# K in four loads, gates fetched two chunks ahead, output splits shared otherwise, and a reordered first stage, in a hybrid attention and retention layer

## The chip, the cores and the metric

The kernel runs on one core of one Trainium2 chip. The metric is the device time of one execution in microseconds (us). The kernel computes on TensorE (matrix products, called PE in the profile), VectorE (DVE), ScalarE (ACT) and GpSimd (POOL). SyncE (SP) issues every DMA, in program order: an issue that has to wait for a buffer holds up all issues behind it.

## The reference

One layer with two parallel branches on the same modulated input, for 1024 latent tokens and 128 context tokens (1152 in all, model width 1024, float32):

```python
mod = silu(cond) @ w_mod + b_mod                  # shift, scale, gate: 3 x 1024
h = layernorm(x) * (1 + scale) + shift
qa, ka, va, za, qr, kr, vr, zr = split(h @ w_in)
# attention, 8 heads: latent queries see 128 cached context keys and 1024 latent keys (rotated)
oa = (softmax(q1 k1') - lam * softmax(q2 k2')) v  # per head, then RMS norm and gain
oa = (oa * silu(za)) @ w_pa
# retention, 8 heads, forwards and backwards in chunks of 128, then layernorm and gain
orr = (orr * silu(zr)) @ w_pr
ga, gr = split(sigmoid(h @ w_gate + b_gate))
y = layernorm(alpha * x + gate * ((ga * oa + gr * orr) @ w_out)) * ln_g + ln_b
```

Outputs are y for both kinds of tokens, and the context's keys, values and retention states. The modulation (shift, scale, gate) differs between latent and context tokens, so each of its 1024 channels has two values, one per row of `cond`.

## The kernel before, in words

Products that must be accurate are made of three: a float32 operand is split into a high part, rounded by ScalarE (`hi_of`), and a low part, the remainder, subtracted by VectorE or GpSimd (`lo_of`); TensorE then adds high x high, high x low and low x high. In profile rows `whi` and `wlo` are the parts of a weight, `Y[:, 0]` and `Y[:, 1]` those of the modulated input h.

All instructions are put out in the order in which the Python code emits them, engine by engine. In the first stage this order is written out by hand. Afterwards a small planner (`Sched`) keeps an estimated clock of TensorE (`sch.t`) and of the other engines (`sch.e`), and lets several generators take turns: a stream of dense jobs (`dense`, one weight tile of 128 output columns each, in three chunks of 384 tokens, 24 matmuls per chunk) fills TensorE while other streams wait. `sch.later` puts a follow-up off until its estimated time; `sch.guard(tag, n)` calls pending follow-ups until fewer than n of that tag are left. Two PSUM buffers (`dn`) take the dense chunks in turn, so TensorE can run one chunk ahead of the engine that empties them.

The stages in order:

- First stage (`phase_h`). Nine tiles of x (128 tokens each) are loaded, normalised, transposed and kept as `xnT`. Beside this the modulation is computed. Channel blocks of 128: scale 0 and 1 and shift 0 and 1 are group 0 of `GS`, scale 2 and 3 group 1, scale 4 to 7 group 2. A group is made by `scale_k(g, k)` on TensorE (one float32 matmul per block k of the input, with the weights as the moving operand), copied by ScalarE (`scale_rows`), transposed, and added to the bias by VectorE (`scale_cols`, into `m1` or `sh`; rows `m<-tp,bm`). The shifts 2 to 7 are made by VectorE alone from row-wise weights (`by_rows`, rows `junk<-wm,scb`). `load_wk(g, k)` loads a group's weights, `load_shift(j)` the row-wise ones; many of these use `p0x`, a ring of six buffers shared with the x tiles, so a load waits until the tile six places earlier has been used. `mod(j)` then makes channel block j of h for all tokens: `hf` on ScalarE, its high part on ScalarE (rows `Y<-hf`), its low part on VectorE (rows `Y<-hf,Y`). After each `mod(k + 1)` TensorE multiplies block k with two weight tiles at once (`k_part`), high x high, low x high, high x low.
- Phase A: projections for retention and attention in the dense stream, with the retention cores beside it. Rotated keys go to DRAM (`Kd`), likewise queries (`Qh`, `Ql`) and values (`Vd`).
- Phase B: attention. For each head h and chunk c (four of 256 latent queries, then one of 128 context queries) `softmax_stream` loads the next chunk's queries (`load_q`), computes the scores into PSUM (`S`), their row maxima (`nm`) and exponentials (`E`). At chunk 1 of a head `load_k(h + 1)` loads the next head's K, 128 partitions x 2 x 1280 floats, into one of two K buffers. `pv_stream` multiplies with V, and `rms` normalises a finished head: a small store to `RSd`, read back broadcast as `rb`. Between these the dense stream runs gates (`g_job`, sigmoid gates stored to `Gd`) and the silu gates (`gate_out`, stored to `ORd` and `OAd` from buffers `goh`, `gol`).
- Phase D: merge. `pr_job(j)` multiplies the gated retention output (tiles `K`, `X`) with `w_pr`, three chunks for each of eight j; VectorE multiplies each chunk by its gate (rows `gt<-gt,dn`) and stores it to `Td`. `merge_in(0, j, c + 1)`, called when chunk c has been evacuated, loads the next gate chunk into one of two `gt` buffers. `pa_job(j)` does the same for attention, with two loads per chunk, the gate (`gt`) and the stored `Td` (`tz`). Beside it `ada_gate` makes the modulation's gate on VectorE (rows `junk<-gw,o_sb`, `gc`).
- Phase E: output. `w_out_split(n)` splits eight pieces of `w_out` into `Y` (no longer needed as input): pieces 0 to 3 are put out just before the last merge chunk, 4 to 7 after it. Even pieces get their low part from GpSimd, odd ones from VectorE. Then matmuls into `e`, the residual, the final layernorm and the stores.

Of the kernel before, what the change touches and what calls it, by code (L numbers as in the profile page):

```python
# [11 lines left out]
F32 = mybir.dt.float32  # L12
F32R = mybir.dt.float32r
AF = mybir.ActivationFunctionType
ALU = mybir.AluOpType
# [3 lines left out]
P = 128  # L19
D = 1024  # L20
KT = D // P
# [3 lines left out]
NH = 8  # L25
CW = 384
NC = NT // CW
# [112 lines left out]
def hybrid_step(ctx: ExitStack, tc: tile.TileContext, I: dict, O: dict):  # L140
# [61 lines left out]
    def dma(out, in_):  # L202
        nc.sync.dma_start(out=out, in_=in_)  # L203
# [159 lines left out]
    def phase_h(first, load_decays, decays_y):  # L363
# [3 lines left out]
        with es:  # L367
# [21 lines left out]
            def load_shift(j):  # L389
                t = wm["shift", j] = p0x("wm")  # L390
                dma(t, I["w_shift"][j])

            GS = ((0, 4), (0, 2), (2, 6))

            def load_wk(g, k):

                a, b = GS[g]
                n = 8 // (b - a)  # L400
                t = p0x("wk") if k == 6 or g == 1 else p0.tile([P, D], F32, tag="wk", name="wk", bufs=3)
                t = t.rearrange("p (k c) -> p k c", k=n)
                dma(t, I["w_scale_k" if g else "w_mod01"][k:k + n, :, a * P:b * P].rearrange("k p c -> p k c"))
                for i in range(n):
                    wm[g, k + i] = t[:, i, :]
# [2 lines left out]
            dma(ident, I["ident"])  # L408
            for i in range(NTILE):
                load_x(i)  # L410
                if i in (2, 4, 6):
                    load_wk(0, i - 2)
                if i == 4:
                    dma(bm, I["b_mod"])
                if i == 6:
                    load_wk(0, 6)
            junk = p0.tile([P, D], mybir.dt.bfloat16, name="junk")
            nc.gpsimd.memset(ones, 1.0 / P)
            nc.gpsimd.memset(mhalf, -0.5)
# [26 lines left out]
            def by_rows(j):  # L446
# [2 lines left out]
                    v_stt(junk, wm["shift", j], 1.0, scb[r], ALU.mult, ALU.mult, accum_out=sh[:, j, r:r + 1])  # L449
                v_ts(sh[:, j, :], sh[:, j, :], bm[:, j:j + 1], None, ALU.add)  # L450

            scale_ps = {}

            def scale_k(g, k):
# [13 lines left out]
            def scale_cols(g):  # L468

                n = GS[g][1] - GS[g][0]  # L470
                rows = rows_of[g]
                tp = psum_now("tp")
                for j in range(n):
                    nc.tensor.transpose(tp[:, 2 * j:2 * j + 2], rows[:, j * P:(j + 1) * P], ident[0:2, 0:2])
                    sch.t += 0.107
                for j0, dst, a, m, one in (((0, m1, 0, 2, 1.0), (2, sh, 0, 2, 0.0)), ((0, m1, 2, 2, 1.0),),
                                           ((0, m1, 4, 4, 1.0),))[g]:
                    c0 = 8 + a if one else a
                    v_stt(dst[:, a:a + m, :], tp[:, 2 * j0:2 * (j0 + m)].rearrange("p (j r) -> p j r", r=2), one,
                          bm[:, c0:c0 + m].rearrange("p (j o) -> p j o", o=1).to_broadcast([P, m, 2]),  # L480
                          ALU.add, ALU.add)
# [15 lines left out]
            for i in range(NTILE):  # L497
                if i + 2 < NTILE:
                    stats(i + 2)
                if i + 1 < NTILE:  # L500
                    normalise(i + 1)
                for g in range(2):
                    tp = psum_now("tp")
                    for k in range(4):
                        kk = g * 4 + k
                        tpose(tp[:, k * P:(k + 1) * P], xt[i][:, kk * P:(kk + 1) * P])
                    act(xnT[:, g * 4:(g + 1) * 4, i * P:(i + 1) * P],
                        tp.rearrange("p (k c) -> p k c", k=4))
                for k in ((), (0, 1), (2,), (3,), (4,), (5,), (6, 7), (), ())[i]:
                    scale_k(0, k)  # L510
                if i == 6:
                    scale_rows(0)
                if i == 7:
                    first[0].split_hi()
                    scale_cols(0)
                    first[1].split_hi()
                if i == 2:
                    first[0].load()
                    first[1].load()
                    load_shift(2)  # L520
                    load_wk(1, 0)
                    load_wk(1, 4)
                    load_shift(3)
                    for k in range(0, KT, 2):
                        load_wk(2, k)

            def mod(j):
                hf = pz.tile([P, NT], F32, tag="o_sb", name="hf", bufs=2)

                def affine(c0, c1, r):  # L530
                    x, m, b = xnT[:, j, c0:c1], m1[:, j, r:r + 1], sh[:, j, r:r + 1]
                    if j:
                        act(hf[:, c0:c1], x, AF.Identity, scale=m, bias=b)
                    else:
                        v_ts(hf[:, c0:c1], x, m, b, ALU.mult, ALU.add, fast=True)

                if j:
                    affine(0, NL, 0)
                    affine(NL, NT, 1)
                    hi_of(Y[:, 0, j, :], hf)  # L540
                else:
                    affine(0, CW, 0)
                    affine(CW, 2 * CW, 0)
                    first[0].split_lo("v")
                    affine(2 * CW, NL, 0)
                    affine(NL, NT, 1)
                    for c in range(NC):
                        hi_of(Y[:, 0, j, c * CW:(c + 1) * CW], hf[:, c * CW:(c + 1) * CW])
                    first[1].split_lo("v")
                if 2 <= j < KT - 2:  # L550
                    by_rows(j + 2)
                lo_of("v", Y[:, 1, j, :], hf, Y[:, 0, j, :])
                if j < 2:
                    by_rows(j + 2)
                if j in (0, 2):
                    load_shift(2 * j + 4 - j)
                    load_shift(2 * j + 5 - j)
                if j == 2:
                    load_decays()

            mod(0)
            for q in range(4):
# [458 lines left out]
    def phase_b():  # L1021
# [11 lines left out]
        def load_k(h):  # L1033

            t = kx.tile([P, 2, 1280], F32R, tag="K", name="K", bufs=2)
            if h < NH:
                dma(t.bitcast(F32), Kd[h])
                Kt[h] = t
            else:
                X[h - NH] = t[:, :, :NT]  # L1040
                if ("gate_out", h - NH, False) in done:
                    load_x(h - NH)

        vseq = [(h, g) for h in range(NH) for g in range(3)]

# [25 lines left out]
        def softmax_stream():  # L1071
            n = 0
            yield sch.t + 20.0
            for si, (h, c) in enumerate(seq):
# [3 lines left out]
                    load_q(*seq[si + 1])  # L1078
                if c == 1:
                    load_k(h + 1)  # L1080
                K = Kt[h]
                QH, QL = Qt[h, c]
                lat = c < 4
# [223 lines left out]

        def merge_in(kind, j, c):

            if c == NC:  # L1310
                j, c = j + 1, 0
            if j == KT:
                kind, j = kind + 1, 0
            if kind == 2 or (kind, j, c) in D_:
                return
            cs = slice(c * CW, (c + 1) * CW)
            g = pz.tile([P, CW], F32, tag="gt", name="gt", bufs=2)
            dma(g, Gd[8 + j if kind == 0 else j, :, cs])
            if kind == 0:
                D_[kind, j, c] = g  # L1320
            else:
                m = pz.tile([P, CW], F32, tag="tz", name="tz", bufs=2)
                dma(m, Td[j, :, cs])
                D_[kind, j, c] = g, m

        def pr_job(j):
            def pre(c):
                merge_in(0, j, c)
                if c:
                    dma(Y[:, c - 1, j, :].bitcast(F32), OAd[c - 1, j])  # L1330

            def evac(c, ps):
                t = D_[0, j, c]
                f = v_stt(t, t, 1.0, ps, ALU.add, ALU.mult)
                dma(Td[j, :, c * CW:(c + 1) * CW], t)
                merge_in(0, j, c + 1)
                return f

            return Job("W", [I["w_pr"][j]], lambda k: X[k], evac, pre=pre,
                       need=lambda k: lambda: done.get(("x", k)))  # L1340
# [9 lines left out]
        def w_out_split(n):  # L1350
            g, k2 = divmod(n, 4)
            r3 = D_.pop(("wo", n)).rearrange("p (k c) -> p k c", k=2)
            hs = Y[:, 0, 2 * k2:2 * k2 + 2, g * 512:(g + 1) * 512]
            ls = Y[:, 1, 2 * k2:2 * k2 + 2, g * 512:(g + 1) * 512]
            f = hi_of(hs, r3)
            lo_of("v" if n % 2 else "p", ls, r3, hs, f)

        def pa_job(j):
            def pre(c):
# [63 lines left out]
        psum_pool(es, "S", 1)  # L1423
        psum_pool(es, "o", 1)
        load_k(0)
        load_q(0, 0)
        sch.run([softmax_stream(), pv_stream(), stream], lambda: "B" in done)
        es.close()
# [180 lines left out]
def _layout(a):  # L1609
# [11 lines left out]
    out["cond"] = np.stack([a["c"][0], a["c_ctx"]]).reshape(2, KT, P).transpose(2, 1, 0)  # L1621
    wm = a["w_mod"][0]
    out["w_mod01"] = np.concatenate([wm[:, D:D + 2 * P], wm[:, :2 * P]], axis=1).reshape(8, P, 4 * P)
    out["w_scale_k"] = wm[:, D + 2 * P:2 * D].reshape(8, P, D - 2 * P)
    out["w_shift"] = wm[:, :D].T.reshape(8, P, D)
    out["w_adag"] = wm[:, 2 * D:].T.reshape(8, P, D)
    out["b_mod"] = _col(a["b_mod"][0])
# [51 lines left out]
```

## Time and profile before

| what | value |
|---|---|
| three timed runs | 1684.17, 1678.61, 1684.23 us; median 1684.17 |
| profiled execution: its time, its span | 1680.3 us, 1678.5 us |
| granted TensorE clock, mean | 0.998 |
| TensorE busy | 1652.8 us in 10515 matmuls |
| ScalarE, VectorE, GpSimd busy | 605.7, 846.0, 780.1 us |
| DMA | 237.36 MB, mean 141 GB/s |

The span runs from the first to the last instruction. In rows of the timeline the columns are start, duration, engine, source line and operation, then out<-in with shapes and the number of instructions merged into the row; the bracket gives the engine's idle time before it and what ended that idle time. Most rows name a helper's line, so the tile names tell which step they belong to. Rows of the chain of waits are start, duration and what the time went to.

### The profile page before, as it was taken

What the parts mean: (1) busy time and instruction counts of PE and PEld (TensorE: products, weight loads), DVE (VectorE), ACT (ScalarE), POOL (GpSimd) and SP (SyncE); (2) the same over time, 40 slices, a digit from 0 to 9 for tenths busy, and PEclk for the clock granted to TensorE, in tenths of its full rate; (3) what the DMA queues carried; (4) which work ended last, traced back from release to release, by engine and by line L of the source; (5) the groups of instructions that cost most, each with busy time, mean ns of one, the idle gap of its engine ahead of it and who ended that gap; (6) DMA issues with size and microseconds to landing.
All of it is one profiled execution on the core that took longest, in us unless ns stands there. A gap on an engine that the chain in (4) does not pass through costs nothing.

```text
span 1678.5 us, 27038 instructions
## 1 busy us (share of the span) xinstructions
PE 1652.8 (98%) x10515; PEld 1606.1 (96%) x10515; DVE 846.0 (50%) x1660; ACT 605.7 (36%) x1136; POOL 780.1 (46%) x544
## 2 busy tenths in 40 slices
PE   8999999999999999999999999999999999999998
PEld 4899999999999999999999999999999999999886
DVE  7735316305606445656556666566555033134676
ACT  6631212221222245455555555555555220012200
POOL 2255427325717556664656466656555321112200
PEclk9999999999999999999999999999999999999999
DMA  9254303521412473635344443435242677854432
GB/s 340 91 170 121 122 16 113 154 69 45 152 56 73 144 237 107 192 104 162 120 115 138 129 140 118 152 99 164 83 151 85 214 266 265 270 175 136 152 126 88
DMA packets 135696, 237.36 MB, mean 141 GB/s; under 512 B 15800, under 2 KB 103312, under 8 KB 134544
## 3 DMA queue, kind: packets, MB, share of 16 engines
q1 hardware_dynamic: 135568, 235.63, 43.8%
q8 instruction: 83, 1.36, 0.3%
q14 instruction: 45, 0.37, 0.1%
HBM read 161.08 MB, written 74.49 MB: 140 GB/s over the span
## 4 chain that ended last, share of the span: by engine, by line
PE 86%; issue 4%; DVE 3%; DMA 3%; POOL 2%; ACT 2%; SPq 1%; DVEq 0%; POOLq 0%; ACTq 0%
PE dn L149 55%; PE S L149 8%; PE o L149 6%; PE e L149 6%; PE a L149 5%; PE tp L153 5%; PE tp L149 1%; DMA gt<-Gd 1%; ACT E L156 1%; SPq L203 1%; DMA xt<-in_x 1%; DVE eps L173 0%; DMA ORd<-goh 0%; DVE r L173 0%; DVE E L173 0%
## 5 line engine op out<-in xcount | busy, mean ns | idle before, releaser
L149 PE MATMUL dn<-Y,whi 128*128 128x384 f32 x3200 | 829.4, 340 | 0.3 <-DVE rt L164 0.3
L149 PEld LDWEIGHTS dn<-Y,whi 128*128 128x128 f32 x3200 | 566.7, 188 | 1.7 <-DVE rt L164 0.6
L149 PE MATMUL dn<-Y,wlo 128*128 128x384 f32 x1600 | 535.8, 336 | 0.0
L185 POOL TENSOR_TENSOR wlo<-raw,whi 128x1024 fp32r<-128x1024 f32 x83 | 199.9, 2411 | 394.7 <-ACT whi L156 388.4
L149 PEld LDWEIGHTS dn<-Y,wlo 128*128 128x128 f32 x1600 | 300.5, 188 | 1.4 <-issue 1.3
L1115 DVE TENSOR_REDUCE nm<-S 128x1 f32<-128x1152 f32 x144 | 178.1, 1237 | 173.2 <-PE S L149 172.9
L189 POOL TENSOR_SCALAR E<-E,r 128x640 f32<-128x640 f32 x64 | 143.7, 2246 | 124.4 <-DVE r L173 85.7
L156 ACT ACTIVATE E<-S,nm 128x1152 f32<-128x1152 f32 x144 | 162.3, 1127 | 79.4 <-DVE nm L1115 74.4
L149 PE MATMUL dn<-whi,Y 128*128 128x256 f32 x864 | 157.6, 283 | 0.4 <-DVE vl L164 0.3
L149 PEld LDWEIGHTS dn<-whi,Y 128*128 128x128 f32 x864 | 134.2, 189 | 0.8 <-DVE vl L164 0.5
L149 PE MATMUL o<-wTh,V 128*128 128x256 f32 x576 | 133.6, 290 | 0.0
L156 ACT ACTIVATE wTh<-tp 128x512 fp32r<-128x512 f32 (+1 forms) x168 | 88.6, 543 | 113.4 <-PE tp L153 109.6
L156 ACT ACTIVATE whi<-raw 128x1024 fp32r<-128x1024 f32 x88 | 92.1, 1055 | 91.6 <-PE dn L149 85.3
L149 PE MATMUL dn<-wlo,Y 128*128 128x256 f32 x432 | 121.4, 281 | 0.0
L164 DVE TENSOR_TENSOR wTl<-tp,wTh 128x512 fp32r<-128x512 f32 (+1 forms) x168 | 99.6, 613 | 25.9 <-ACT wTh L156 25.9
L185 POOL TENSOR_TENSOR E<-E 128x640 f32<-128x640 f32 x64 | 100.4, 1568 | 5.3
L149 PE MATMUL S<-K,QH 128*128 128x384 f32 (+1 forms) x400 | 94.7, 340 | 6.3 <-ACT E L156 6.3
L149 PEld LDWEIGHTS o<-wTh,V 128*128 128x128 f32 x576 | 99.4, 188 | 0.2 <-ACT wTh L156 0.2
L149 PE MATMUL S<-K,QL 128*128 128x384 f32 (+1 forms) x400 | 92.6, 335 | 0.0
L153 PE MATMUL tp<-ident,E 128*128 128x128 f32 x584 | 86.8, 272 | 0.0
L173 DVE SCALAR_TENSOR_TENSOR gt<-gt,dn 128x384 f32<-128x384 f32 x48 | 26.6, 554 | 118.8 <-DMA gt<-Gd 61.9
L169 DVE TENSOR_SCALAR KD<-tp,kdec 128x256 f32<-128x256 f32 (+1 forms) x48 | 16.1, 409 | 139.5 <-PE tp L153 139.5
(203 smaller groups left out, 2463.0 us busy)
## 6 DMA issues: line engine op xcount, KB each, us to landing
K<-Kd SPq DMA_DIRECT2D x8, 1280.0 KB, 7.5
Gd<-gt SPq DMA_DIRECT2D x48, 192.0 KB, 2.6
V<-Vd SPq DMA_DIRECT2D x24, 384.0 KB, 4.1
gt<-Gd SPq DMA_DIRECT2D x48, 192.0 KB, 2.5
Y<-OAd SPq DMA_DIRECT2D x16, 576.0 KB, 4.0
raw<-in_w_gate SPq DMA_DIRECT2D x16, 512.0 KB, 4.3
QH<-Qh SPq DMA_DIRECT2D x64, 128.0 KB, 3.3
QL<-Ql SPq DMA_DIRECT2D x64, 128.0 KB, 2.9
```

Of the source, the lines that this page charges most:

```text
L149: nc.tensor.matmul(out, lhsT=lhsT, rhs=rhs, start=start, stop=stop)
L153: nc.tensor.transpose(out, in_, ident)
L156: nc.scalar.activation(out, in_, func, **kw)
L164: nc.vector.tensor_tensor(out, a, b, op=op)
L169: nc.vector.tensor_scalar(out, a, s1, s2, op0=op0, **kw)
L173: nc.vector.scalar_tensor_tensor(out, a, s, b, op0=op0, op1=op1, **kw)
L185: nc.gpsimd.tensor_tensor(out, a, b, op=op)
L189: nc.gpsimd.tensor_scalar(out, a, s1, None, op0=op0)
L203: nc.sync.dma_start(out=out, in_=in_)
L1115: nc.vector.tensor_reduce(nm[:, m:m + 1], ps[:, :nb, :kw], axis=AX.XY, op=ALU.max, negate=True)
```

## The change

- First stage: x tiles 7 and 8 are now loaded ahead of group 0's last weights, and group 0's matmuls begin one tile earlier. Group 2 covers scale 4 to 6 only. Scale 7 is made like the shifts, by VectorE from row-wise weights (`load_scale`, `scale_by_rows`), put out at the end of `mod(3)`.
- K of the next head is loaded in four quarters of 320 columns, one at each of the chunks 1 to 4.
- `merge_in` runs two chunks ahead in the `pr_job` half; its odd chunks use buffers of the tag `tz`.
- The low parts of the output weights: pieces 2, 5 and 7 by GpSimd, the others by VectorE.

```diff
-            GS = ((0, 4), (0, 2), (2, 6))
+            def load_scale():
+                t = wm["scale", KT - 1] = p0x("wm")
+                dma(t, I["w_scale7"])
+            GS = ((0, 4), (0, 2), (2, 5))
...
-                t = t.rearrange("p (k c) -> p k c", k=n)
+                t = t[:, :n * (b - a) * P].rearrange("p (k c) -> p k c", k=n)
...
                 load_x(i)
-                if i in (2, 4, 6):
+                if i in (2, 4, 6, 8):
                     load_wk(0, i - 2)
                 if i == 4:
                     dma(bm, I["b_mod"])
-                if i == 6:
-                    load_wk(0, 6)
...
+            def scale_by_rows():
+                j = KT - 1
+                for r in range(2):
+                    v_stt(junk, wm["scale", j], 1.0, scb[r], ALU.mult, ALU.mult, accum_out=m1[:, j, r:r + 1])
+                v_ts(m1[:, j, :], m1[:, j, :], bm[:, 8 + j:9 + j], 1.0, ALU.add, ALU.add)
...
-                                           ((0, m1, 4, 4, 1.0),))[g]:
+                                           ((0, m1, 4, 3, 1.0),))[g]:
...
-                for k in ((), (0, 1), (2,), (3,), (4,), (5,), (6, 7), (), ())[i]:
+                for k in ((0, 1), (2,), (3,), (4,), (5,), (6,), (7,), (), ())[i]:
                     scale_k(0, k)
...
+                if j == 1:
+                    load_scale()
                 if j == 2:
                     load_decays()
+                if j == 3:
+                    scale_by_rows()
...
             if h < NH:
-                dma(t.bitcast(F32), Kd[h])
                 Kt[h] = t
+                load_k_part(h, 0)
...
+        def load_k_part(h, q):
+            if h < NH:
+                ks = slice(q * 320, (q + 1) * 320)
+                dma(Kt[h][:, :, ks].bitcast(F32), Kd[h, :, :, ks])
...
                 if c == 1:
                     load_k(h + 1)
+                elif c:
+                    load_k_part(h + 1, c - 1)
...
-            if c == NC:
-                j, c = j + 1, 0
+            if c >= NC:
+                j, c = j + 1, c - NC
...
-            g = pz.tile([P, CW], F32, tag="gt", name="gt", bufs=2)
+            if kind == 0 and (NC * j + c) % 2:
+                sch.guard("silu", 1)
+                sch.guard("tz", 1)
+                g = pz.tile([P, CW], F32, tag="tz", name="gt", bufs=2)
+            else:
+                g = pz.tile([P, CW], F32, tag="gt", name="gt", bufs=2)
...
                 merge_in(0, j, c)
+                if (j, c) == (0, 0):
+                    merge_in(0, 0, 1)
...
-                merge_in(0, j, c + 1)
+                merge_in(0, j, c + 2)
...
-            lo_of("v" if n % 2 else "p", ls, r3, hs, f)
+            lo_of("p" if n in (2, 5, 7) else "v", ls, r3, hs, f)
...
         load_k(0)
+        for q in range(1, 4):
+            load_k_part(0, q)
```

Outside the core's program the column-wise scale weights lose their last 128 columns, which are passed transposed as `w_scale7`.

More of the change, by code (lines that the diff above doesn't have):

```diff
@@ L1623, in _layout @@
     out["w_mod01"] = np.concatenate([wm[:, D:D + 2 * P], wm[:, :2 * P]], axis=1).reshape(8, P, 4 * P)
-    out["w_scale_k"] = wm[:, D + 2 * P:2 * D].reshape(8, P, D - 2 * P)
+    out["w_scale_k"] = wm[:, D + 2 * P:2 * D - P].reshape(8, P, D - 3 * P)
+    out["w_scale7"] = wm[:, 2 * D - P:2 * D].T
     out["w_shift"] = wm[:, :D].T.reshape(8, P, D)
```

## The prediction

> **What bounds the kernel now.** I read the page's engine shares first, then its chain, then TensorE's waits, then busy time by stage.
>
> ```profile
> PE 1652.8 (98%) x10515; PEld 1606.1 (96%) x10515; DVE 846.0 (50%) x1660; ACT 605.7 (36%) x1136; POOL 780.1 (46%) x544
> PE 86%; issue 4%; DVE 3%; DMA 3%; POOL 2%; ACT 2%; SPq 1%; DVEq 0%; POOLq 0%; ACTq 0%
> ```
>
> TensorE is busy for 98% of the span and carries 86% of the chain that ended last. No other engine is above 50%. So the change can only pay where it takes matmul work away or ends one of TensorE's few waits. This is the view of whom TensorE waited for; columns: total us, times, longest.
>
> ```profile
> PE S L149 <- ACT E L156: 6.3, 5, 1.6
> PE dn L149 <- DVE gt L173: 1.4, 4, 0.6
> PE e L149 <- POOL Y L185: 1.1, 2, 0.8
> PE tp L153 <- DVE gc L164: 0.9, 1, 0.9
> ```
>
> The four rows make 9.7 us, and each belongs to a place that the diff edits: the attention scores (S), the merge (dn waiting for gt, and tp), the output (e). That, and the first stage, is all there is to win. A group's waits are counted as idle time, and a matmul whose modelled end overlaps the next start hides part of a wait, so I also count matmuls by stage.
>
> ```profile
> 590.00:1310.00 720.00, 712.96 (x4635) 705.75 (x4634) 426.38 (x705) 381.61 (x735) 442.48 (x278) 1.00 0.43 134
> 1310.00:1367.00 57.00, 57.00 (x331) 56.91 (x330) 7.92 (x9) 14.70 (x23) 20.25 (x14) 1.00 0.76 268
> 1367.00:1400.00 33.00, 32.84 (x190) 32.52 (x189) 11.59 (x18) 3.65 (x4) 7.19 (x3) 1.00 0.73 244
> 1400.00:1428.00 28.00, 26.48 (x148) 25.10 (x146) 12.77 (x22) 2.12 (x2) 4.81 (x2) 1.00 0.80 272
> ```
>
> Columns: stage, its length, busy time of PE, PEld, DVE, ACT, POOL with their counts, granted clock, DMA share, GB/s. The undisturbed stage 1310 to 1367 runs 331 matmuls in 57 us, 5.81 per us. The clock is 1.00 in all four.
>
> **First stage.** Three edits: tiles 7 and 8 of x are loaded ahead of the last block of group 0's weights; group 2 of the scale columns shrinks from four column blocks to three; the eighth block is done by `scale_by_rows` on VectorE, after mod(3).
>
> ```profile
> 10.00:20.00 10.00, 9.14 (x48) 4.28 (x46) 8.21 (x20) 7.82 (x13) 5.16 (x10) 1.00 1.04 400
> 19.91 1.29 DVE L181 BATCH_NORM_STATS2 st<-xt 128x6 f32<-128x512 f32 x2 [1.62 <-DMA xt<-in_x]
> 30.37 1.89 PE L149 MATMUL tp<-wk,sc 128*2 128x256 f32 x8 [1.28 <-ACT xnT L156]
> 39.02 7.03 PE L149 MATMUL tp<-wk,sc 128*2 128x512 f32 x16
> 44.27 1.22 DVE L173 SCALAR_TENSOR_TENSOR junk<-wm,scb 128x1024 bf16<-128x1024 f32 x1
> 46.09 0.59 ACT L156 ACTIVATE rows<-tp 2x512 f32<-2x512 f32 x1 [3.13 <-PE tp L149]
> 46.80 0.23 DVE L169 TENSOR_SCALAR sh<-sh,bm 128x2 f32<-128x2 f32 x1
> 49.42 1.36 DVE L164 TENSOR_TENSOR Y<-hf,Y 128x1152 fp32r<-128x1152 f32 x1 [2.40 <-ACT Y L156]
> 50.70 0.16 DVE L173 SCALAR_TENSOR_TENSOR m<-tp,bm 128x8 f32<-128x8 f32 x1
> 50.89 1.63 ACT L156 ACTIVATE hf<-xnT,sh,m 128x1024 f32<-128x1024 f32 x2 [1.50 <-DVE m L173]
> 61.95 1.36 DVE L164 TENSOR_TENSOR Y<-hf,Y 128x1152 fp32r<-128x1152 f32 x1 [1.39 <-ACT Y L156]
> 63.79 0.51 PE L149 MATMUL dn<-Y,whi 128*128 128x384 f32 x2
> ```
>
> Earlier tiles: VectorE waits 1.62 us for tile 7. The queue moves 400 GB/s, so one 512 KB load ahead of it costs 524288 B / 400 GB/s = 1.3 us; tile 7 and tile 8 come that much sooner and the weights that much later, behind them. The scale matmuls move one tile earlier and stand in front of the next transposes, so I take 1.2 us (ends 0 and 1.62).
>
> Narrower matmuls: 256 columns took 1.89 / 8 = 0.236 us, 512 took 7.03 / 16 = 0.439; half-way, 384 columns, 0.338. Sixteen of them save 16 x 0.101 = 1.6 us of TensorE. One tiny transpose goes too.
>
> So group 2's matmuls end 2.8 us sooner: 46.05 becomes 43.2. From there the order is fixed by the code. ScalarE copies the rows (46.09), then makes hf and Y of block 3; VectorE subtracts (49.42 to 50.78, having waited 2.40 for that Y); only then comes m (50.70 in the row), for which hf of block 4 waits (1.50). Between the subtraction and m the change puts `scale_by_rows`: two products of 1.22 us, their accumulator reads and a small add of 0.23 us. The same set in the trace runs from 44.27 to 47.03, 2.76 us. Hence m is ready at 50.86 - 2.8 + 2.76 = 50.8, as before. From m on, ScalarE's pairs of hf and Y run without a break from 50.89 up to VectorE's last subtraction at 61.95, which ends at 63.31, and the next TensorE products (63.79) cannot start much before: 0.48 us is all the slack there is. What TensorE saved turns into waits at blocks 4 and 7. I put this stage at -0.1 us. The ends: -2.8 if m is not held up, +1.1 if the tiles win nothing (46.05 - 1.6, then 2.76).
>
> The extra 512 KB of the row-wise weights replaces four times 128 KB of the column-wise ones; SP issues it behind the fourth and fifth shift loads, and it is wanted only after block 3's subtraction. It takes a slot of the ring, so the seventh shift load waits on SP until the products of the third shift are done, and the small decay loads and the next weights queue behind it; all are wanted later than 50 us, and the queue is emptying by then. Nothing waits on these: 0; if the decay loads came late, part of the +1.1 above would be theirs.
>
> **K in four loads.** The 1280 KB of the next head's K go out as quarters with chunks 1 to 4 of the current head, so bytes stay, and SP gets three more issues of about 0.6 us per head, 21 in all, on a queue that TensorE waits for nowhere in the list above.
>
> ```profile
> K<-Kd SPq DMA_DIRECT2D x8, 1280.0 KB, 7.5
> 701.89 0.59 SPq L203 DMA_DIRECT2D K<-Kd  x1
> 702.58 7.25 DMA ORd<-goh
> 709.85 0.49 ACT L156 ACTIVATE goh<-dn 128x384 f32<-128x384 f32 x1 [1.68 <-DMA ORd<-goh]
> 711.60 0.79 PE L149 MATMUL S<-K,QH 128*128 128x384 f32 x3 [1.57 <-ACT E L156]
> 1138.96 0.58 SPq L203 DMA_DIRECT2D K<-Kd  x1
> 1142.23 0.30 SPq L203 DMA_DIRECT2D RSd<-rst  x1
> 1146.26 0.81 SPq L203 DMA_DIRECT2D rb<-RSd  x2
> 1149.64 1.02 POOL L185 TENSOR_TENSOR o_sb<-o_sb,rb 128x384 f32<-128x384 f32 x1 [4.60 <-DMA rb<-RSd]
> 1156.32 0.79 PE L149 MATMUL S<-K,QH 128*128 128x384 f32 x3 [1.45 <-ACT E L156]
> ```
>
> Two of the five score waits trace back to a K load in flight. At 701.89 K goes out; the gate's store behind it takes 7.25 us; ScalarE waits 1.68 us for that buffer, its exponential comes late and TensorE stands 1.57 us. At 1138.96 K goes out; the tiny RSd store is not there for the reads until 1146.26, GpSimd waits 4.60 us, and TensorE stands 1.45 us. A quarter in the queue is a quarter of that delay (7.5 / 4 = 1.9 us), less than either chain needs to stay hidden. Together 3.0 us; I take -2.6, since something later must end each wait. Ends: -3.0, and 0 if other transfers fill the queue just as long.
>
> That DMA time is not what TensorE waits for stands in the stage's row above: a DMA share of 0.43 from 590 to 1310. One rule speaks against this edit. The Trainium skill, DMA: Bandwidth & Descriptors, section Bandwidth, says to batch transfers to at least 1 MiB, because each carries a fixed part. By its fit (an estimate from that page) the whole K takes 2.0 + 1310720 / 436000 = 5.0 us and a quarter 2.75, so four take 11.0, 6 us of transfer more per head; a quarter would still be there in time, so the sum by it is the same. The trace's whole load lands in 7.5 us, not 5.0; no run so far shows a quarter.
>
> **Merge gates two chunks ahead.** Now each gate chunk is fetched when the previous one has been merged, one chunk (24 matmuls, 24 / 5.81 = 4.1 us) before it is wanted. At 5.81 per us the 148 matmuls of 1400 to 1428 need 25.5 us and the 190 of 1367 to 1400 need 32.7: 2.5 + 0.3 = 2.8 us lost. The wait rows name 1.4 us for the gate and 0.9 us for gc, which is queued on VectorE behind the late gate products. With two chunks of lead both should go. Odd chunks use the tz buffers; the gates that used these ended long before, so the two guards find nothing, and the Td store that frees a buffer is two chunks old. Only the first fetch of the second half waits on SP for the newest Td store, with nothing urgent behind it. I take -2.6; ends -2.8 and, if gc still waits and one gate wait stays, -1.0.
>
> **Output splits.** Blocks 0, 4, 6 move to VectorE, 5 and 7 to GpSimd, 2 stays on GpSimd.
>
> ```profile
> 29.08 1.22 DVE L164 TENSOR_TENSOR wlo<-raw,whi 128x1024 fp32r<-128x1024 f32 x1
> 1569.51 5.72 POOL L185 TENSOR_TENSOR Y<-raw,Y 128x1024 fp32r<-128x1024 f32 x2 [18.41 <-ACT Y L156]
> 1570.42 2.57 DVE L164 TENSOR_TENSOR Y<-raw,Y 128x1024 fp32r<-128x1024 f32 x1 [1.34 <-ACT Y L156]
> 1572.91 3.40 DVE L164 TENSOR_TENSOR Y<-wo,Y 128x1024 fp32r<-128x1024 f32 x1
> ```
>
> Blocks 0 and 2 take GpSimd 5.72 us, while a split alone takes VectorE 1.22 us; run beside GpSimd's it took 2.57 and 3.40. After: block 0 ends at about 1570.7, in time for TensorE's second output matmul, block 1 at 1571.9; block 2 starts on GpSimd as soon as ScalarE has its high part, with no block 0 ahead of it. Of the 1.1 us of e waits about 0.3 stays. In the second half the last split still ends before its matmuls. I take -0.8; ends -1.1 and +0.5 (block 7 late).
>
> **Sum.** -0.1 - 2.6 - 2.6 - 0.8 = -6.1 us. The profiled execution took 1680.3 us around a span of 1678.5, which gives 1674.2. It lies 3.9 us under the median of 1684.17; the four executions shown (1684.17, 1678.61, 1684.23, 1680.3) average 1681.8. Against that average the forecast is 1675.7 us, 0.36% less. Half a per cent, 8.4 us, is about what a measurement of this kernel can tell from no change.
>
> **Rivals.**
>
> (a) The first stage does pay: m is not held up and its -2.8 counts. For it: VectorE's 2.40 us idle shows room. Against: the order of the code puts m behind. Time: 1675.7 - 2.7 = 1673.0.
>
> (b) The score waits move instead of going. The planner that orders phases A and B starts, by the cost formulas in its helpers, with its TensorE clock 1.8 us earlier and VectorE's 2.5 us later, so the interleaving changes; three of the five score waits already have nothing to do with K. If K's 2.6 us come back elsewhere the result is 1678.3; if one or two further such waits (1.6 us each) arise, 1681.5.
>
> (c) Slower: the last quarter of K lands late. It is issued behind the Q loads of the next head's first chunk, three chunks later than now.
>
> ```profile
> V<-Vd SPq DMA_DIRECT2D x24, 384.0 KB, 4.1
> 1026.43 1.22 SPq L203 DMA_DIRECT2D QL<-Ql  x2
> 1032.58 0.77 PE L149 MATMUL S<-K,QH 128*128 128x384 f32 x3
> ```
>
> The shortest lead is here: 1032.58 - 1027.65 = 4.9 us for the issue (0.6) and the landing. The nearest transfer in size, V, lands in 4.1 us, so 4.7 us just fits. Seven heads cross this point. To end 8.4 us slower it must eat 6.1 + 8.4 = 14.5 us, 2.1 per head: a landing of some 6.4 us after issue at a head like this one. Time 1690 at that point. The other loads in flight are few there, so I hold it unlikely; one head losing 1 us is likelier.
>
> (d) The edits do nothing measurable: the buffers come free as late as before. 1681.8.
>
> **How the numbers follow.** Forecast (within 2 us) 0.45, (a) 0.17, (b) 0.22, (c) 0.06, (d) 0.10. The gain lies 2.3 us short of the half per cent and the four executions differ by 5.6, so a third of the forecast's chance counts as faster, with (a) and a little of (b): 0.15 + 0.17 + 0.03 = 0.35. Slower is (c), 0.06. The rest, 0.59, is within. The range runs from (a) on the lowest of the executions, 1678.6 - 8.8 = 1669.8, less 1, to (d): 1669 to 1682; what it leaves out is (c) and the far ends of (a) and (b).
>
> **What would show it.** First stage: the DVE row m at about 50.8 and the last Y subtraction still ending near 63.3, TensorE waiting for ACT Y or DVE Y there; a saving would show as both 2 to 3 us earlier. K: no store over 5 us behind a K load, RSd read back within 2 us, S waits 3 us instead of 6.3. Merge: the waits for gt and gc gone, 163 matmuls in 28 us. Output: e waits under 0.4. The forecast is wrong if S waits grow, above all with a K quarter as releaser, or if new waits appear in phase A.

## The result

| set of runs | before, median | changed, median | ratio, 95% interval |
|---|---|---|---|
| first, 6 runs of each | 1682.68 us | 1671.05 us | 0.9935 [0.9914, 0.9956] |
| second, 6 runs of the changed kernel | 1680.97 us | 1670.18 us | 0.9936 [0.9922, 0.9950] |

The change gains 0.65%: 11.6 us in the first set and 10.8 in the second, where 6.1 had been forecast. The first median lies 4.7 us below the forecast of 1675.7, inside the range, and in the case "faster by over 0.5%", which had 0.35 against 0.59 for "within". One of the ten runs of the kernel before in the second set took 2318.99 us at a granted clock of 0.655; its median counts that run, the ratio does not. The profiled execution of the changed kernel took 1670.85 us around a span of 1669.1, close to its median; the profiled one of before lay 2.4 us under its median. So the two traces differ by only 9.4 us. Starts of the same TensorE instruction in both traces (us) show where these lie. Each trace holds one stretch of half clock, described further down, so that these cancel:

| TensorE instruction | before | changed | difference | this part |
|---|---|---|---|---|
| first score matmul | 594.91 | 593.96 | -0.95 | first stage -0.95 |
| last score matmul | 1294.98 | 1290.45 | -4.53 | attention -3.58 |
| first merge matmul | 1367.21 | 1362.69 | -4.52 | 0.0 |
| transpose of gc | 1428.60 | 1420.41 | -8.19 | merge -3.67 |
| output matmul behind the second split | 1571.96 | 1562.74 | -9.22 | splits -1.03 |
| end of the span | 1678.5 | 1669.1 | -9.4 | -0.2 |

### The profile page after: what moved, and what is told of

The parts are those of the page before. It is cut to its first block, busy times and chain, and to the rows that moved or that the text cites. A ratio compares the mean times of both kernels' runs of the same rounds, so it can differ in the third digit from the quotient of the medians.

```text
span 1669.1 us, 27056 instructions
## 1 busy us (share of the span) xinstructions
PE 1649.2 (99%) x10514; PEld 1605.3 (96%) x10514; DVE 847.3 (51%) x1666; ACT 606.0 (36%) x1136; POOL 780.0 (47%) x543
## 4 chain that ended last, share of the span: by engine, by line
PE 92%; DVE 3%; ACT 2%; DMA 1%; POOL 1%; issue 1%; SPq 0%; DVEq 0%; ACTq 0%; POOLq 0%
PE dn L149 62%; PE S L149 8%; PE o L149 6%; PE e L149 6%; PE tp L153 5%; PE a L149 4%; PE tp L149 1%; ACT Y L156 1%; DMA wk<-in_w_mod 1%; ACT hf L156 0%; DVE eps L173 0%; ACT E L156 0%; DVE E L173 0%; DVE nm L1135 0%; DVE r L173 0%
```

## The profile after

The engine shares, and whom TensorE waited for (total us, times, longest), in the changed kernel:

```profile
PE 1649.2 (99%) x10514; PEld 1605.3 (96%) x10514; DVE 847.3 (51%) x1666; ACT 606.0 (36%) x1136; POOL 780.0 (47%) x543
PE S L149 <- ACT E L156: 3.3, 3, 1.2
PE dn L149 <- ACT Y L156: 1.3, 1, 1.3
PE dn L149 <- DVE rt L164: 0.8, 1, 0.8
PE e L149 <- POOL Y L185: 0.3, 1, 0.3
```

The waits for gt and gc are gone, S is down from five waits to three, e from 1.1 us to 0.3; a new wait of 1.3 us for Y stands in the first stage. The timeline there:

```profile
18.51 1.28 DVE L181 BATCH_NORM_STATS2 st<-xt 128x6 f32<-128x512 f32 x2 [0.23 <-DMA xt<-in_x]
28.34 1.89 PE L149 MATMUL tp<-wk,sc 128*2 128x256 f32 x8 [1.28 <-ACT xnT L156]
36.99 5.32 PE L149 MATMUL tp<-wk,sc 128*2 128x384 f32 x16
49.52 0.16 DVE L173 SCALAR_TENSOR_TENSOR m<-tp,bm 128x6 f32<-128x6 f32 x1
52.59 0.61 PE L149 MATMUL dn<-Y,whi 128*128 128x384 f32 x2 [1.28 <-ACT Y L156]
60.76 1.36 DVE L164 TENSOR_TENSOR Y<-hf,Y 128x1152 fp32r<-128x1152 f32 x1 [1.39 <-ACT Y L156]
75.23 0.61 PE L149 MATMUL dn<-Y,whi 128*128 128x384 f32 x2 [0.79 <-DVE rt L164]
```

VectorE's wait for x tile 7 fell from 1.62 us to 0.23, and TensorE reaches group 1 at 28.34 instead of 30.37, 2.0 us sooner. The sixteen narrower matmuls take 5.32 us instead of 7.03. Yet m comes only 1.2 us sooner than before (49.52, was 50.70), and so does the last subtraction (60.76, was 61.95). The place where before had K in flight:

```profile
K<-Kd SPq DMA_DIRECT2D x32, 320.0 KB, 3.8
699.58 0.60 SPq L203 DMA_DIRECT2D K<-Kd  x1
705.76 0.48 ACT L156 ACTIVATE goh<-dn 128x384 f32<-128x384 f32 x1
707.57 0.74 PE L149 MATMUL S<-K,QH 128*128 128x384 f32 x3
1139.69 0.29 SPq L203 DMA_DIRECT2D RSd<-rst  x1
1140.94 0.81 SPq L203 DMA_DIRECT2D rb<-RSd  x2
1144.22 1.02 POOL L185 TENSOR_TENSOR o_sb<-o_sb,rb 128x384 f32<-128x384 f32 x1 [1.72 <-DMA rb<-RSd]
```

ScalarE no longer waits for the gate's store, S follows without a wait, and the small RSd store is read back 1.25 us after its issue instead of 4.03. A quarter of K lands in 3.8 us at the median. For the merge, its first and last TensorE row before, the same two after, and the two windows of the changed kernel:

```profile
1367.21 0.51 PE L149 MATMUL dn<-K,whi 128*128 128x384 f32 x2
1428.60 0.28 PE L153 MATMUL tp<-ident,gc 128*16 128x128 f32 x1 [0.93 <-DVE gc L164]
```

```profile
1362.69 0.51 PE L149 MATMUL dn<-K,whi 128*128 128x384 f32 x2
1420.41 0.27 PE L153 MATMUL tp<-ident,gc 128*16 128x128 f32 x1
1362.00:1395.00 33.00, 33.00 (x192) 33.00 (x192) 11.88 (x21) 3.65 (x4) 8.31 (x3) 1.00 0.83 284
1395.00:1420.00 25.00, 25.00 (x146) 25.00 (x145) 13.60 (x22) 2.12 (x2) 5.85 (x2) 1.00 0.82 269
```

The same 333 matmuls take 57.72 us instead of 61.39, and TensorE is busy in all of it.

## Experiments

Eight of the eleven runs below were executed once each. The kernel before, executed once beside them, took 1678.73 us with four of them (tile order, eighth scale, K spread, merge) and 1684.76 with the other four, so single spans of the same kernel differ by several us. What is said of these eight therefore rests on places in the traces, and spans are given beside them. The other three were timed several times, side by side. Except where it says otherwise, an edit is made to the kernel before.

**The first stage: tile order alone, eighth scale alone.** The first run keeps the scale columns on TensorE:

```diff
-                if i in (2, 4, 6):
+                if i in (2, 4, 6, 8):
...
-                if i == 6:
-                    load_wk(0, 6)
...
-                for k in ((), (0, 1), (2,), (3,), (4,), (5,), (6, 7), (), ())[i]:
+                for k in ((0, 1), (2,), (3,), (4,), (5,), (6,), (7,), (), ())[i]:
```

> Of the first stage only the new order of loads and group 0's matmuls one tile earlier; scale 7 stays on TensorE. Theory V (VectorE's chain of Y subtractions sets the stage's end, and every saving ahead of it is carried through): first float32r product at about 30.2 us instead of 32.2, m at 48.8 instead of 50.7, last Y subtraction at 59.9 instead of 61.95, and the second dense job about 2 us earlier; span 1676.5. Theory G (what the changed kernel gave back between 46 and 76 us, 2.6 of 3.6 us, is a wait that any earlier start meets): only 1 us is left at 76 us, span 1677.5.

The second run has only the other half:

```diff
-            GS = ((0, 4), (0, 2), (2, 6))
+            GS = ((0, 4), (0, 2), (2, 5))
...
+                if j == 1:
+                    load_scale()
...
+                if j == 3:
+                    scale_by_rows()
```

> Of the first stage only scale 7 by VectorE; order of the tile loads as before. Theory V: the narrower matmuls end 1.6 us sooner, but the 2.7 us of row-wise products stand ahead of m, so m comes at 50.7 - 1.6 + 2.7 = 51.8 us, the last Y subtraction starts at 63.0, and the stage ends 0.6 to 1.1 us later than before: span 1679.1 to 1679.6. Theory G (the 1.6 us are a saving of their own): m not later than 50.7, stage 1 to 1.6 us earlier, span 1677.

The row of m and the first matmul of the block behind the stage (76.23 before), first with the tile order alone, then with the scale alone:

```profile
48.92 0.16 DVE L173 SCALAR_TENSOR_TENSOR m<-tp,bm 128x8 f32<-128x8 f32 x1
74.44 0.62 PE L149 MATMUL dn<-Y,whi 128*128 128x384 f32 x2 [0.30 <-DVE rt L164]
```

```profile
51.80 0.16 DVE L173 SCALAR_TENSOR_TENSOR m<-tp,bm 128x6 f32<-128x6 f32 x1
77.51 0.62 PE L149 MATMUL dn<-Y,whi 128*128 128x384 f32 x2 [0.78 <-DVE rt L164]
```

The tile order gains 1.8 us at both places, the scale on VectorE loses 1.1 at m and 1.3 at the end of the stage, although it saves TensorE 1.7 us of matmuls. In the executions in which this stage was not edited, and without half clock in it, the second of these starts lies between 76.20 and 76.50, so both effects are clear of what varies. The spans were 1679.7 and 1681.8 us, where 1676.5 and 1679.1 to 1679.6 had been expected. That both are longer is due to later places, though neither was edited: in the first the wait behind the K load at 712 us was 3.09 us instead of 1.57 and the merge took 62.69 us instead of 61.39; in the second the merge took 63.04.

**The whole change with the scale back on TensorE.**

```diff
-            GS = ((0, 4), (0, 2), (2, 5))
+            GS = ((0, 4), (0, 2), (2, 6))
...
-                if j == 1:
-                    load_scale()
...
-                if j == 3:
-                    scale_by_rows()
```

> The changed kernel with scale 7 back on TensorE (group 2 has four blocks again), all else as changed. Theory V: the stage keeps the 2.0 us of the earlier tiles and loses the 2.7 us of VectorE's products: 1 us faster than the changed kernel's profile, span 1668.1. Theory G: the narrower matmuls were worth 1.6 us, span 1670.7.

```profile
48.80 0.16 DVE L173 SCALAR_TENSOR_TENSOR m<-tp,bm 128x8 f32<-128x8 f32 x1
74.33 0.61 PE L149 MATMUL dn<-Y,whi 128*128 128x384 f32 x2 [0.30 <-DVE rt L164]
```

The edit is to the changed kernel. The stage ends 0.9 us sooner than there (75.23). The span, 1669.2 us, doesn't show it, because this execution held one stretch of half clock more (below). It was timed again, beside the changed kernel:

> The changed kernel again, as the yardstick for the two runs beside it. From its profile: span near 1669.1 us, 9 to 12 us below the kernel before; three waits of S on E of 1.0 to 1.4 us near 674, 1110 and 1162 us, m at 49.5 and the last subtraction of Y at 60.8 us. Both theories on the seventh scale and on eps leave this run as it was.

> The changed kernel with the seventh scale back on TensorE and ScalarE. VectorE-chain theory: the first stage ends about 0.9 us earlier than in the changed kernel, so the time is 0.9 us shorter, 0.05%, which lies within what five rounds can tell apart (interval about 0.2%). Rival, the scale on VectorE does win its 1.3 to 1.6 us of TensorE time: 1.5 us longer than the changed kernel.

Medians 1670.18 us for the changed kernel and 1669.55 with the scale back; ratios to before 0.9936 [0.9922, 0.9950] and 0.9931 [0.9919, 0.9944]. The sign agrees with the traces, the size is too small for this measurement.

**K in quarters, three ways.** Spread over chunks 1 to 4 as in the change:

```diff
-                dma(t.bitcast(F32), Kd[h])
+                load_k_part(h, 0)
...
+                elif c:
+                    load_k_part(h + 1, c - 1)
```

> Only K in four loads. Theory Q (a whole K in the queue holds up small transfers; two score waits come from it): the waits of 1.57 us at 711 and 1.45 at 1156 go, S waits fall from 6.3 to about 3.3 us, RSd is read back within 1.6 us of its store at every head; span 1675.2 (3.3 less). Rival M (the waits move): S waits stay above 5 us, span 1677 to 1679.

All four at chunk 1, so that only the size of the loads changes:

```diff
                 if c == 1:
                     load_k(h + 1)
+                    for q in range(1, 4):
+                        load_k_part(h + 1, q)
```

> Before, with K in four quarters, but all four issued at chunk 1, so that the same 1280 KB are queued at once. Theory Q (what counts is how many bytes are queued ahead of a small store): nothing is won, the two waits of 1.57 and 1.45 us stay, RSd is read back 4 to 6 us after its store where K is in flight, S waits about 6.3 us, span 1678 to 1679. Rival S (smaller loads let other transfers in between): S waits about 3.3 us, span 1675.2.

All four at chunk 4, so that only their time changes:

```diff
-                if c == 1:
+                if c == 4:
                     load_k(h + 1)
+                    for q in range(1, 4):
+                        load_k_part(h + 1, q)
```

> Before, with all four quarters of the next head's K at chunk 4, behind the queries of its first chunk. This prices the lead that the last quarter has: 4.9 to 9.1 us from the end of the query issues to the first scores. Four issues of 0.6 us and the landing of 1280 KB (5.0 to 7.5 us) need 7 to 9 us. If the lead is as read from the rows, TensorE waits for K at two heads some 2 to 4 us each and at four heads 0 to 2 us: +4 to +12 us, less the 3.3 us of the two old waits, span 1679 to 1687, with DMA K among the releasers of S. If leads do not matter: span 1675.

TensorE's waits for S with the quarters spread:

```profile
PE S L149 <- ACT E L156: 3.3, 3, 1.2
```

In one burst, with the timeline at the two old places:

```profile
PE S L149 <- ACT E L156: 10.0, 6, 3.0
703.70 2.57 SPq L203 DMA_DIRECT2D K<-Kd  x4
713.10 0.49 ACT L156 ACTIVATE goh<-dn 128x384 f32<-128x384 f32 x1 [3.12 <-DMA ORd<-goh]
714.85 0.79 PE L149 MATMUL S<-K,QH 128*128 128x384 f32 x3 [3.00 <-ACT E L156]
1147.82 0.30 SPq L203 DMA_DIRECT2D RSd<-rst  x1
1151.81 0.80 SPq L203 DMA_DIRECT2D rb<-RSd  x2
```

All at chunk 4:

```profile
PE S L149 <- DMA K<-Kd: 5.4, 6, 2.0
PE S L149 <- ACT E L156: 3.3, 3, 1.2
767.31 0.44 PE L149 MATMUL S<-K,QH 128*128 128x384 f32 x1 [2.00 <-DMA K<-Kd]
```

Spread, the waits at 711 and 1156 us go, and the span is 1676.0 us. In a burst they stay (3.00 us at 714.85; RSd read back after 3.99 us), the waits for S grow from 6.3 to 10.0 us, and the span is 1683.4 (1.6 of it from one more stretch of half clock than before had, below): no gain was expected, but by these waits there is a loss. What counts is the amount of K in flight ahead of a small urgent store, not the size of one load. Moved to chunk 4, the two old waits go too, presumably because nothing urgent stands behind, but K itself comes late: 5.4 us of waits on it, span 1684.1 us (some 1.5 of it from half clock beyond what before had). So rival (c) was a real mechanism; in the change, with only the last quarter at chunk 4, no wait for K is left. The stretch from the first to the last score matmul says the same without the other stages: 697.1 us with K spread, 703.8 in a burst, 704.0 all at chunk 4, and 699.8 to 701.2 in the five executions with K whole.

**The merge alone.**

```diff
-                merge_in(0, j, c + 1)
+                merge_in(0, j, c + 2)
```

> Only the gates two chunks ahead. Theory L (each gate chunk comes late, and gc behind it): no wait for gt nor gc, the stretch from 1390 to 1430 runs at 5.8 matmuls per us, 3.8 us less, span 1674.7. Rival N (only the named waits go): 1.4 + 0.9 = 2.3 us less, span 1676.2.

```profile
1368.74 0.51 PE L149 MATMUL dn<-K,whi 128*128 128x384 f32 x2
1426.45 0.27 PE L153 MATMUL tp<-ident,gc 128*16 128x128 f32 x1
```

Again 57.7 us instead of 61.4. The span is 1676.3, close to the 1676.2 of the rival that only the named waits (2.3 us) go; but the stretch itself shows 3.67 us, and the score wait behind K at 712 us, not edited, was 2.62 us here instead of 1.57. In all six profiled executions with two chunks of lead this stretch took 57.72 us. In the seven with one chunk it took 60.69 to 63.04, 61.99 on average: a fetch that comes late is late by another amount each time.

**The output splits alone.**

```diff
-            lo_of("v" if n % 2 else "p", ls, r3, hs, f)
+            lo_of("p" if n in (2, 5, 7) else "v", ls, r3, hs, f)
```

> Only the output splits shared otherwise. Theory: the wait for block 0's low part goes, 0.3 us of the wait for block 2 stays, 1.0 us less; span 1677.5. Rival (the wait moves to block 7, which is now GpSimd's): e waits of 0.5 us or more around 1585 us, span 1678 to 1679.

```profile
PE e L149 <- POOL Y L185: 0.3, 1, 0.3
```

From the gc transpose to the end of the span this kernel takes 248.72 us, before 249.92, and nothing waits for block 7. In all executions this part takes 248.66 to 248.74 us with the new shares and 249.85 to 250.71 with the old ones. The span, 1679.5 us against an expected 1677.5, hides it: this execution held one stretch of half clock more than before's, and its merge took 62.35 us.

**The three S waits that are left.** In the timeline of the changed kernel:

```profile
672.47 2.45 POOL L185 TENSOR_TENSOR wlo<-raw,whi 128x1024 fp32r<-128x1024 f32 x1 [5.17 <-ACT whi L156]
672.60 2.33 DVE L173 SCALAR_TENSOR_TENSOR eps<-s 128x1 f32<-128x1 f32 x1
674.86 0.28 DVE L1135 TENSOR_REDUCE nm<-S 128x1 f32<-128x128 f32 x1
675.68 0.33 PE L149 MATMUL S<-K,QH 128*128 128x128 f32 x1 [1.23 <-ACT E L156]
```

VectorE's eps has one element per partition and takes 0.15 us at the median. Here it takes 2.33 and ends with GpSimd's wlo, at 674.9; nm, E and S come late in turn. The test moves eps to ScalarE, on top of the version with the scale back:

```diff
-                        v_stt(e2, s[:, 0:1], LN_EPS, s[:, 0:1], ALU.mult, ALU.mult)
+                        nc.scalar.activation(e2, s[:, 0:1], AF.Square, scale=math.sqrt(LN_EPS))
+                        sch.op("dve", 0.12 + 1 / 960, None, True)
```

The last line keeps the planner's clock as it was.

> As the run with the seventh scale back, and the small product eps of the softmax statistics moved from VectorE to ScalarE (a Square with a scale, the same value). Theory: the three S waits that are left (1.39, 1.39 and 0.95 us) come from eps on VectorE, which took 2.33 us instead of 0.15 while GpSimd ran wlo for 2.45 us; with eps on ScalarE no S wait over 0.5 us stays near 674, 1110 and 1162 us, and the span is 3.3 to 3.7 us shorter than with the scale back alone, near 1664. Rival: the next small VectorE operation of that chain is held in the same way, or ScalarE's own queue delays eps as long, the three waits stay at 1 us or more, and the time stays within 1 us of the run beside it.

The tile eps on ScalarE (line, count; shortest, median, longest in ns), and the longest of TensorE's waits in this kernel, among which S no longer appears:

```profile
L1110 ACT ACTIVATE eps<-s x72: 186/199/222, 604.2 to 1285.6; 128x1 f32<-128x1 f32 x72
PE a L149 <- DMA ident<-in_ident: 3.5, 1, 3.5
PE tp L149 <- ACT xnT L156: 1.3, 1, 1.3
PE dn L149 <- DVE vl L164: 0.3, 1, 0.3
```

The median is 1664.02 us, ratio to before 0.9898 [0.9885, 0.9912]: 5.5 us below the version beside it (1669.55), with intervals apart, and the best version of this study. The expectation of 3.3 to 3.7 was too small. Between the two traces, neither of which has half clock there, the stretch from the first to the last score matmul is 4.9 us shorter (694.9 to 690.0). From start to start the three waits give 3.7 of it (1.39, 1.39 and 0.96), and 0.6 comes from a wait for wTl at 893 us that this edit did not aim at.

## Why the prediction was right or wrong

The four mechanisms and all signs held; the sum of -6.1 us was too small because all four terms were sized too small, by 3.4 us together in the pair of traces. That the time still fell into the range is in part luck: its lower end had been set by rival (a), whose mechanism did not come about.

- First stage, -0.1 predicted, -0.95 in the traces. That VectorE's products stand ahead of m and give TensorE's saving back was right: the saving of 3.6 us at 45 us (the matmul starting at 45.46 before and 41.83 after) has shrunk to 1.0 at 76 us. "m at 50.8, last subtraction near 63.3" was missed by 1.2 us. The term that failed is the tile order, sized at 1.2 us from one load at 400 GB/s; it brought 2.0. VectorE's 1.4 us less of waiting is one part; the rest I put down to TensorE, which no longer holds scale matmuls back to the last tiles; that is argued, not shown. Undoing the scale on VectorE shows -0.9 more.
- K, -2.6 predicted with an end of -3.0; -3.6 in the pair of traces, and -4.1 between averages (from first to last score matmul 700.6 us in the five executions with K whole, 696.5 in the five with the quarters spread and eps where it was). Both waits went, as said. They are worth more than their rows: from start to start TensorE lost 1.73 us at 709.69 and 1.61 at 1154.59, where the rows have 1.57 and 1.45. And this wait is not fixed: with K whole it was 1.5 to 3.3 us from start to start in five executions, with before's 1.73 second from the bottom. The rule of the Trainium skill quoted in the prediction (DMA: Bandwidth & Descriptors, section Bandwidth: transfers of at least 1 MiB) speaks of throughput; here its price was hidden, as a quarter that landed in 3.8 us at the median was in time at every head. The fit on the same page of the Trainium skill, stated there for transfers issued from GpSimd, had given an estimate of 2.75 us.
- Merge, -2.6 predicted with an end of -2.8; -3.67 in the pair, and 61.99 - 57.72 = 4.3 against the average. The step that failed is the count by windows: a window counts a matmul that crosses its border, so 331, 190 and 148 hold 329, 188 and 146 starts. The loss read there was 0.3 us too small in this way, the last 0.6 us before the gc transpose lay outside the windows, and the profiled execution was a mild one.
- Splits, -0.8 predicted with an end of -1.1; -1.03 up to the output matmul behind the second split and -1.26 to the end of the span. The row was again a lower bound: the wait for e that went has 0.82 us in its row and cost 0.99 from start to start.
- What the pair of traces leaves out of the measured gain comes from the execution of before that it holds, a mild one. With averages over executions the four terms are -1.1 (the start behind the first stage: 76.31 us in the five of 76.20 to 76.50, and 75.23), -4.1, -4.3 and -1.4 (the part from the gc transpose on), together -10.9, against 10.8 and 11.6 measured. The base of the forecast, 1681.8 us, was off by at most 0.9 (the medians of before are 1682.68 and 1680.97).

Of the 2.8 us of rival (a) about 1.0 came. Rival (b) did not happen: from the first score matmul on, TensorE runs the same 6544 matmuls in the same order in both traces, and no score wait is new. Nor did (c) in the changed kernel, and (d) is excluded by the interval.

## What the runs showed of the hardware that I had not expected

**Half clock behind a wait.** The mean clock of 0.998 hides short stretches. Columns as in the windows above (the clock is the third from the end); before, right behind its S wait at 676 us, and just after it; then the version with the scale back at the same place; then K all at chunk 4, behind its K waits:

```profile
677.70:680.90 3.20, 3.20 (x12) 3.20 (x11) 2.48 (x4) 1.25 (x4) 3.12 (x3) 0.50 0.54 137
681.20:684.40 3.20, 3.20 (x23) 3.16 (x23) 2.46 (x3) 0.40 (x1) 1.17 (x2) 1.00 0.73 244
```

```profile
677.70:680.90 3.20, 3.20 (x22) 3.16 (x21) 3.17 (x3) 0.02 (x1) 3.20 (x3) 1.00 0.79 239
```

```profile
768.90:775.50 6.60, 6.60 (x25) 6.41 (x26) 1.92 (x3) 2.81 (x5) 2.37 (x1) 0.50 0.45 88
```

For 3.4 us (6.8 in the last) the clock is 0.50 and TensorE does half the matmuls: 12 instead of 23 in 3.2 us, a loss of some 1.6 us. In 13 profiled executions, leaving out the start and the tail of the span, there are 16 such stretches, and each begins between 0.2 us before and 0.9 us behind the end of a TensorE wait of at least 1.27 us (waits here from start to start, less the time of the matmul before). Of 56 waits of 1.38 us or more, 15 have one so close behind; the double stretch follows a wait of 2.2 us and one of 1.3 in a row. So such a wait costs on average 16 / 56 x 1.6 = 0.5 us more than itself.

Which waits are hit can be read from 24 equal ones, those of 1.4 us near 676 and 1115 us in every kernel but the one with eps moved. The traces record each change of the granted clock, and within a trace the changes between the start and the tail lie a whole number of steps of 3.413 us apart (669.01 us, 196 steps, from the first full clock to the stretch in before). Counted on this grid, the 11 waits that end 2.5 to 3.0 us into a step have half clock in the next step, and the 13 that end elsewhere have none. Waits of another kind or length fit less well: one of 1.6 us ahead of the gc transpose ended 3.0 us into a step and had none. Where a wait falls on the grid changes from execution to execution.

With eps moved, no such wait is left after 30 us, and no stretch lies there. Its four timed runs spread over 1.7 us, the six of the changed kernel over 3.5 and 5.1 in the two sets, and those of before over 9.6 in the first; but the six of the version with the scale back, which has the two waits, spread over only 2.0, so the spread is no proof. This is a regularity in these traces; no run was made to set it off on purpose, though the K waits at 767 and 769 us were new and brought a new stretch. The Trainium skill, TensorE: Matmul & The Clock Gate, Part 1, has the clock halved after an idle window of about 3.4 us that runs freely: length, ratio and the free grid agree with these traces, but here 1.4 us of waiting was enough.

**A tiny VectorE instruction held by GpSimd.** The eps above took 2.33 us instead of 0.15 and ended with GpSimd's operation. In the trace of the changed kernel 8 of its 72 instances took 0.96 to 2.34 us. Each of the 8 began beside a two-input operation of GpSimd (TENSOR_TENSOR) and ended within 0.02 us of it. Beside GpSimd's operation on one tile and a scalar it was not held, as 30 us later:

```profile
701.99 2.37 POOL L189 TENSOR_SCALAR E<-E,r 128x640 f32<-128x640 f32 x1 [0.19 <-DVE r L173]
702.52 0.15 DVE L173 SCALAR_TENSOR_TENSOR eps<-s 128x1 f32<-128x1 f32 x1
```

The same holds for all 49 instances beside such an operation; two late in a small TENSOR_TENSOR of GpSimd were not held either. The Trainium skill, SBUF — State Buffer, section SBUF: two separate sides, says that VectorE with two inputs in SBUF and GpSimd share a port which one holds for a whole instruction, as long as GpSimd's operation reads SBUF. The 8 instances agree, the 49 do not. Moving this one line of code, with its 72 instances, gained 5.5 us.

## What to carry to other kernels

Look for what stands behind a large transfer in its queue: a load that nobody waits for can still be what delays a small store or read that somebody does, and then spreading it over time helps while cutting it up alone does not. Size a wait from start to start of the waiting engine's instructions over several executions: in these traces its row was a lower bound, a fetch that came late varied, and some waits of 1.3 us or more on TensorE were followed by half clock. A saving on the bounding engine that lengthens the chain it next waits for is given back: ask for each moved piece of work whose turn it now stands ahead of.
